# Small generators at every second unit in the linear-attention stage of a decoder step

## The chip, the cores and the metric

The kernel runs on one core of one Trainium2 chip. The time is the device time of one execution in microseconds (us), and the median over several runs counts. The profile comes from one execution of its own; times in it are counted from the start of its span.

The core has engines that run side by side, each with its own queue of instructions in fixed order: TensorE (PE in the profile; its weight loads are PEld), VectorE (DVE), ScalarE (ACT), GpSimd (POOL) and SyncE (SP), which issues DMA transfers. An instruction that has to wait holds up everything behind it on its engine.

## What is computed

One inference step of a hybrid decoder layer: an input projection that feeds two kinds of attention heads, stick-breaking attention (8 heads, with a paged cache for 8 decoding sequences of 4 tokens) and gated linear attention (4 heads or groups), a gate for each branch, and an output projection. The part that matters here is linear attention:

```python
def gla_chunk(S, q, k, v, g):
    b = jnp.cumsum(g, axis=2)
    diff = b[:, :, :, None, :] - b[:, :, None, :, :]
    decay = jnp.where(causal[None, None, :, :, None], jnp.exp(jnp.minimum(diff, 0.0)), 0.0)
    attn = jnp.einsum('bhtk,bhsk,bhtsk->bhts', q, k, decay)
    o = jnp.einsum('bhts,bhsv->bhtv', attn, v) + jnp.einsum('bhtk,bhkv->bhtv', q * jnp.exp(b), S)
    b_last = b[:, :, -1:, :]
    S_new = (jnp.exp(b_last[:, :, 0, :])[..., None] * S
             + jnp.einsum('bhsk,bhsv->bhkv', k * jnp.exp(b_last - b), v))
    return S_new, o
```

The prompt has 1024 tokens and 16 meta tokens, with 32 sample tokens behind them: T = 1072 columns. D_MODEL is 2048, a group has 128 key and 256 value columns.

## The kernel before

All projections are exact to float32 by three products: weights and activations are split into a high and a low half (wh, wl; hh, hl), and wh·hh, wh·hl and wl·hh (L288 to L290) add up in an accumulator. `inproj` (L277) projects one block of 128 columns: 8 weight chunks of 2 × 128 rows, and for each chunk 3 pieces of the 1072 tokens (384, 384, 304 columns), 6 matmuls a piece. After each piece it calls `W.beat()`: these 6 matmuls, about 1 us of TensorE, are one **unit**, and one `inproj` is 24 units. `weight_chunk` brings each chunk in: SyncE issues the load of wr, ScalarE casts it to wh (L183), VectorE subtracts to get wl (L184). After the last chunk `evac` empties the three accumulators (a pool of three buffers) through ScalarE.

All other work is woven into the projections by a `Weaver`. Work is written as Python generators; each yields the number of units until it goes on, and they lie in a heap by the unit in which they are due. `beat()` counts one unit and lets every generator that is due emit its next step, so its instructions land in the queues between two pieces of the projection. There is no other planner: the order in which instructions are emitted is the order in each engine's queue (only the weight chunks and `evac` are marked urgent).

The linear-attention stage (L644 to L1016) runs, for each of the four groups g, `inproj` for gk, gq and twice gv, 96 units in all. The three pieces of gk and gq are put into place by ScalarE copies (`place`, L672 to L680). Woven into it are, for each group:

- `decay`: for three token chunks, al on TensorE (L730), then ny, e (L733 to L737) on ScalarE and VectorE, and scans on VectorE into cb. It waits 5 units ahead of a chunk and 1 behind it.
- `own`: the diagonal blocks P_d (L754) and their masking at (L756), waiting 3 units after each.
- `level`: seven levels (64 to 1), each with X on VectorE and ScalarE (L780 to L784, the exponential in L782), 6 units later its products P (L789) and masked copies (L793, L799). `inside` starts one every 4 units.
- `inside`: after the levels, 3 units later eb, ke, k·ke (L825); 7 units later the transposes of k by token (`by_token`, L859, tr_k) and `packed` (trp_k L848, pk L849 to L851). `gv_tok` does the same for v (tr_v).
- `chunks`: 9 chunks with the state update U, the outputs o, ow (L922 to L936), then 8 samples with km (L958), Us (L961), sn (L963). Each chunk starts a `chunk_out` after 1 unit, which scales ow, waits 3 units, transposes it (otr) and writes it out through gst; at the end `samples_out` waits 9.

The next group's decay starts, and its chunks follow, once kd is there. Tiles of stages come from pools: the transposes' PSUM pool (tag tr) has one buffer, that of the P tiles two, and the stage pool `stg` seven, shared by ny, e, graw, rep, km, ow, gst, sn and the gate's gs and gx.

Two lasting generators run along: `z_feed` (VectorE products with cached key pages, L386, 2048 of them over the kernel, one step every 2 units), and `weight_forms` (L400 to L416). The groups are followed by two gate groups (`gate_group`) and `W.drain()` at L1016. The projection of further gate columns goes on after that beside the paged decode's beginning: there spn, spb (L1079), Cs (L1097) and Cn (L1101) belong to the new keys, ds_l (L1047) and a scan (L1121) to the cached ones.

Of the kernel before, what the change touches and what calls it, by code (L numbers as in the profile page):

```python
# [50 lines left out]
class Weaver:  # L51
# [1 line left out]


    def __init__(self):
        self.now, self.n, self.live, self.heap, self.mark = 0, 0, 0, [], None

    def spawn(self, gen, delay=0, lasting=False):
        heapq.heappush(self.heap, (self.now + delay, self.n, gen, lasting))
# [2 lines left out]

    def beat(self):
        self.now += 1
        while self.heap and self.heap[0][0] <= self.now:
            _, _, gen, lasting = heapq.heappop(self.heap)
            self.live -= not lasting
            d = next(gen, None)
            if d is not None:
                self.spawn(gen, d, lasting)  # L70
# [12 lines left out]
def hybrid_step(ctx: ExitStack, tc: tile.TileContext, x_prompt, x_sample, cache_k, cache_v, state_gla,  # L83
# [23 lines left out]
    W = Weaver()  # L107
# [331 lines left out]
    def gate_group(g):  # L439
        def evac(c, ps, lo, hi):  # L440
            x = stage(f"gx{g}_{c}")
            evacs.append(act.copy(x[:, :hi - lo], ps).ins)  # L442
            W.spawn(gate_rest(g, lo, hi, x), 1)
        inproj(C_SG + g * P if g < 8 else C_GG + (g - 8) * P, evac, META, f"g{g}")
# [198 lines left out]


    with tc.tile_pool(name="gp", bufs=1) as gp, tc.tile_pool(name="gps", bufs=1, space=PSUM) as gps:
        XW = 9 * P
        ones = gp.tile([P, 1], F32, name="ones")
        pool.memset(ones[:], 1.0)
# [8 lines left out]
        def view(t, off, *dims):  # L657
            a = t if isinstance(t, bass.AP) else t[:]
            return bass.AP(tensor=a.tensor, offset=a.offset + off, ap=[list(a.ap[0])] + [list(d) for d in dims])
# [56 lines left out]
        def xtile(nm):  # L716
            return gp.tile([P, XW], F32, tag="X", bufs=4, name=nm)

# [29 lines left out]
        def own(g, at, kt, qt):  # L748

            for c0 in (0, EB):  # L750
                ps = gps.tile([P, 512], F32, tag="P", bufs=2, name=f"P{g}_d_{c0}")
                for i in range(4):
                    cs = slice(c0 + i * P, c0 + (i + 1) * P)
                    mm(ps[:, i * P:(i + 1) * P], kt[:, cs], qt[:, cs], start=True, stop=True)  # L754
                j = 0 if c0 == 0 else 4
                vec.tensor_tensor(at[:, j:j + 4, :], ps[:].rearrange("p (a t) -> p a t", t=P),  # L756
                                  ident[:].unsqueeze(1).to_broadcast([P, 4, P]), ALU.mult)
                yield 3
            ps = gps.tile([P, 512], F32, tag="P", bufs=2, name=f"P{g}_d_8")
            cs = slice(1024, T)  # L760
            mm(ps[:48, :48], kt[:, cs], qt[:, cs], start=True, stop=True)
            vec.tensor_tensor(at[:48, 8, :48], ps[:48, :48], ident[:48, :48], ALU.mult)
# [39 lines left out]
        def inside(g, at, kt, qt, cb, res):  # L802

            yield from own(g, at, kt, qt)
            for m in (64, 32, 16, 8, 4, 2, 1):
                W.spawn(level(g, m, at, kt, qt, cb))
                yield 4
            yield 3
            eb = xtile(f"eb{g}")
            act.activation(eb[:, :T], cb[:, :T], AF.Exp, scale=-1.0 / 16.0)  # L810
            vec.tensor_tensor(qt[:, :T], qt[:, :T], eb[:, :T], ALU.mult)
            ebl = gp.tile([P, 17], F32, tag="ebl", name=f"ebl{g}")
            vec.tensor_copy(view(ebl, 1, (-1, 2), (2, 4)), view(eb, 0, (EB + P - 1, 2), (P, 4)))
            vec.tensor_copy(ebl[:, 8:9], eb[:, REAL - 1:REAL])
            vec.tensor_copy(ebl[:, 9:17], eb[:, REAL:T].rearrange("p (b t) -> p b t", t=NT)[:, :, NT - 1])
            ke = xtile(f"ke{g}")
            full = ((EB, 2), (P, 4), (1, P))
            vec.tensor_tensor(view(ke, 0, *full), view(cb, 0, (EB + P - 1, 2), (P, 4), (0, P)), view(cb, 0, *full),
                              ALU.subtract)
            for lo, hi, w in ((1024, REAL, 16), (REAL, T, NT)):  # L820
                cv = cb[:, lo:hi].rearrange("p (c t) -> p c t", t=w)
                vec.tensor_tensor(ke[:, lo:hi].rearrange("p (c t) -> p c t", t=w),
                                  cv[:, :, w - 1:w].to_broadcast([P, (hi - lo) // w, w]), cv, ALU.subtract)
            act.activation(ke[:, :T], ke[:, :T], AF.Exp, scale=-1.0 / 16.0)
            vec.tensor_tensor(kt[:, :T], kt[:, :T], ke[:, :T], ALU.mult)  # L825
            rep_ = three(kt[:, REAL:T], f"k{g}")
            yield 7
            kd = xtile(f"kd{g}")
            pk = gp.tile([96, P], F32R, tag="pk", name=f"pk{g}")
            by_token(kt, kd, (0, 4), col, f"k{g}")  # L830
            yield 1
            by_token(kt, kd, (4, 4), col, f"k{g}")
            yield 1
            by_token(kt, kd, (8, 1), col, f"k{g}")
            res["kd"], res["ebl"], res["pk"] = kd, ebl, pk
            yield 1
            packed(rep_, pk[:], 2, f"k{g}")

        def three(src, nm):

            rep = stage(f"rep_{nm}")[:, :96]
            vec.tensor_copy(rep.rearrange("p (a t) -> p a t", a=3), src.unsqueeze(1).to_broadcast([P, 3, NSMP]))
            return rep

        def packed(rep, dst, lo, nm):

            ps = gps.tile([P, 512], F32, tag="tr", name=f"trp_{nm}")
            nc.tensor.transpose(ps[:96, :P], rep, ident[:])  # L848
            act.copy(dst, ps[:96, :P])  # L849
            ls = slice(32 * lo, 32 * lo + 32)  # L850
            vec.tensor_tensor(dst[ls], ps[ls, :P], dst[ls].bitcast(F32), ALU.subtract)  # L851

        def by_token(src, dst, gr, at_, nm):
            c0, nch = gr
            ps = gps.tile([P, 512], F32, tag="tr", name=f"tr_{nm}_{c0}")
            for i in range(nch):
                c = c0 + i
                r = P if c < 8 else 48
                nc.tensor.transpose(ps[:r, i * P:(i + 1) * P], src[:, at_(c):at_(c) + r], ident[:])  # L859
                if r < P:  # L860
                    act.copy(dst[:r, c * P:(c + 1) * P], ps[:r, i * P:(i + 1) * P])
            nf = nch if c0 + nch < 9 else nch - 1
            if nf:
                act.copy(dst[:, c0 * P:(c0 + nf) * P], ps[:, :nf * P])
# [115 lines left out]
        for g in range(GH):  # L980
# [14 lines left out]
            pool.memset(at[:48, 8, 48:76], 0.0)  # L995
            res = {}
            W.spawn(inside(g, at, kt, qt, cbs[g], res), 2)
            gv = []
            pv = gp.tile([96, DV], F32R, tag="pv", name=f"pv{g}")
# [14 lines left out]
        for g in range(3, 5):  # L1014
            gate_group(g)
        W.drain()  # L1016

    dk_cm.__exit__(None, None, None)

# [2 lines left out]
    with tc.tile_pool(name="dp", bufs=2) as dp, tc.tile_pool(name="dps", bufs=1, space=PSUM) as dps:  # L1022
# [150 lines left out]
        def sample_out(b, osb):  # L1173

            ps = dps.tile([P, 512], F32, tag="oT", name=f"oT{b}")
            for h in range(4):
                nc.tensor.transpose(ps[:, h * P:(h + 1) * P], osb[:, h * P:(h + 1) * P], ident[:])
            a = ps[:]
            for f in range(2):
                own = bass.AP(tensor=a.tensor, offset=a.offset + 48 * f, ap=[list(a.ap[0]), [P + NT, 4], [1, NT], [64, 2]])  # L1180
                vec.tensor_reduce(osmp[:, 4 * f:4 * f + 4, b * NT:(b + 1) * NT], own, mybir.AxisListType.X, ALU.add)
            return
            yield
# [359 lines left out]
def build(arrays_by_name):  # L1543
    import concourse.bacc as bacc
    nc = bacc.Bacc("TRN2", target_bir_lowering=False, num_devices=1, dynamic_dma_scratch_size=256)
    arrays, args = {}, []
    for name in _INS:
        a = arrays_by_name[name]
        arrays[f"in_{name}_dram"] = a
        args.append(nc.dram_tensor(f"in_{name}_dram", a.shape, mybir.dt.from_np(a.dtype), kind="ExternalInput").ap())  # L1550
    for i, shape in enumerate(_OUTS):
        args.append(nc.dram_tensor(f"out_{i}_dram", shape, F32, kind="ExternalOutput").ap())
    with tile.TileContext(nc) as tc:
        hybrid_step(tc, *args)
    return nc, arrays
# [8 lines left out]
```

## Time and profile before

| | us |
|---|---|
| median of 3 runs | 2113.27 (2111.09 to 2113.43) |
| the profiled execution | 2108.24 |
| its span, first to last instruction | 2106.5 |
| TensorE busy in it | 2056.2 (98%) |
| VectorE busy | 1569.7 (75%) |
| ScalarE busy | 991.8 (47%) |
| granted TensorE clock, mean | 0.995 |

The profiled execution is 0.24% below the median, and 1.7 us of it lie around the span. A matmul's duration in the timeline includes its passage through the array, so consecutive matmuls overlap; the distance between two starts is what one costs. A number in brackets at the end of a row is the idle time of the engine before it and what ended it. Line numbers with "L" are those of the kernel before; in the changed kernel they are 2 to 4 higher.

### The profile page before, as it was taken

To read this page: it belongs to the slowest core of one execution; us is meant where nothing else is said; L and a number is where in the kernel's file an instruction comes from. 1 tells how busy PE (TensorE), PEld (TensorE's weight loads), DVE (VectorE), ACT (ScalarE), POOL (GpSimd) and SP (SyncE) were. 2 spreads that over 40 slices of the span, in tenths; PEclk is the share of its full clock that TensorE was granted. 3 is DMA by queue.
4 is the path that set the end of the run, shared out by engine and by line. 5 is a ranking of instruction groups with operands and counts; after the bars stand their busy time and mean duration, and the time that the engine had idled before them with its cause. 6 is when DMAs were issued, how large, how long until landed. Compare 5 with 4: busy or idle time off the path is not lost.

```text
span 2106.5 us, 43298 instructions
## 1 busy us (share of the span) xinstructions
PE 2056.2 (98%) x12546; PEld 1868.4 (89%) x12546; DVE 1569.7 (75%) x6593; ACT 991.8 (47%) x2539; POOL 80.9 (4%) x298
## 2 busy tenths in 40 slices
PE   5999999999999999999999999999999999999998
PEld 4999999999999989999899898998888888777776
DVE  6368888889888889899889988877544347453576
ACT  7346555565655547423535335353444326332342
POOL 0000000100000000020000000000000000000000
PEclk9999999999999999999999999999999999999999
DMA  6234443544444353544353444434776666352485
GB/s 200 72 103 123 132 131 100 144 118 121 139 124 126 108 145 102 156 132 117 110 138 104 123 129 113 107 85 135 244 234 219 224 218 201 127 159 75 130 279 186
DMA packets 378505, 301.96 MB, mean 143 GB/s; under 512 B 50073, under 2 KB 318777, under 8 KB 378265
## 3 DMA queue, kind: packets, MB, share of 16 engines
q1 hardware_dynamic: 376072, 298.91, 48.1%
q8 instruction: 99, 1.62, 0.3%
q14 instruction: 142, 1.16, 0.2%
q10 hardware_dynamic: 2192, 0.27, 0.1%
HBM read 241.75 MB, written 57.31 MB: 142 GB/s over the span
## 4 chain that ended last, share of the span: by engine, by line
PE 84%; DMA 6%; DVE 6%; ACT 2%; issue 1%; SPq 0%; DVEq 0%; POOL 0%; ACTq 0%; POOLq 0%
PE acc_g L288 4%; PE acc_g L290 4%; PE b L1471 4%; PE acc_g L289 4%; PE b L1472 4%; PE b L1473 4%; PE acc_k L288 3%; PE acc_gv L288 3%; PE acc_k L289 3%; PE acc_q L288 3%; PE acc_k L290 3%; PE acc_gv L290 3%; PE acc_gv L289 3%; PE acc_q L289 3%; PE acc_q L290 3%; PE acc_v L288 3%
## 5 line engine op out<-in xcount | busy, mean ns | idle before, releaser
L386 DVE SCALAR_TENSOR_TENSOR jk<-kp,qb 128x128 f32<-128x128 f32 x2048 | 591.6, 289 | 38.9 <-DMA qb<-qsd 1.5
L288 PE MATMUL acc_g<-hT,wh_g 128*128 128x368 f32 (+2 forms) x768 | 251.7, 328 | 0.8 <-ACT gx L442 0.8
L290 PE MATMUL acc_g<-hT,wl_g 128*128 128x368 f32 (+2 forms) x768 | 248.4, 323 | 0.0
L289 PE MATMUL acc_g<-hT,wh_g 128*128 128x368 f32 (+2 forms) x768 | 247.9, 323 | 0.0
L1471 PE MATMUL b<-ring,f 128*128 128x512 f32 x416 | 165.7, 400 | 3.2 <-ACT b L1344 2.0
L386 DVE DVE_READ_ACCUMULATOR jk<-kp,qb 128x1 f32 x2048 | 166.9, 81 | 0.0
L1309 DVE TENSOR_TENSOR ring<-wr,ring 128x512 fp32r<-128x512 f32 x104 | 70.6, 690 | 128.7 <-ACT ring L1308 128.3
L1472 PE MATMUL b<-ring,f 128*128 128x512 f32 x416 | 162.8, 391 | 0.7 <-DVE ring L1309 0.5
L1473 PE MATMUL b<-ring,f 128*128 128x512 f32 x416 | 162.4, 390 | 0.0
L288 PEld LDWEIGHTS acc_g<-hT,wh_g 128*128 128x128 f32 x768 | 145.1, 189 | 12.4 <-issue 10.2
L290 PEld LDWEIGHTS acc_g<-hT,wl_g 128*128 128x128 f32 x768 | 144.9, 189 | 2.0 <-issue 2.0
L289 PEld LDWEIGHTS acc_g<-hT,wh_g 128*128 128x128 f32 x768 | 145.1, 189 | 0.7
L1308 ACT CAST ring<-wr 128x512 fp32r<-128x512 f32 x104 | 64.4, 622 | 159.0 <-DMA wr<-in_w_out_dram 80.6
L288 PE MATMUL acc_gv<-hT,wh_gv 128*128 128x384 f32 (+1 forms) x384 | 129.6, 338 | 0.0
L288 PE MATMUL acc_k<-hT,wh_k 128*128 128x378 f32 (+1 forms) x384 | 127.8, 333 | 0.0
L288 PE MATMUL acc_q<-hT,wh_q 128*128 128x368 f32 (+2 forms) x384 | 125.5, 327 | 0.0
L289 PE MATMUL acc_k<-hT,wh_k 128*128 128x378 f32 (+1 forms) x384 | 125.5, 327 | 0.0
L290 PE MATMUL acc_k<-hT,wl_k 128*128 128x378 f32 (+1 forms) x384 | 125.3, 326 | 0.0
L290 PE MATMUL acc_gv<-hT,wl_gv 128*128 128x384 f32 (+1 forms) x384 | 125.2, 326 | 0.0
L289 PE MATMUL acc_gv<-hT,wh_gv 128*128 128x384 f32 (+1 forms) x384 | 124.6, 325 | 0.0
L289 PE MATMUL acc_q<-hT,wh_q 128*128 128x368 f32 (+2 forms) x384 | 123.8, 322 | 0.0
L290 PE MATMUL acc_q<-hT,wl_q 128*128 128x368 f32 (+2 forms) x384 | 123.6, 322 | 0.0
(441 smaller groups left out, 5398.3 us busy)
## 6 DMA issues: line engine op xcount, KB each, us to landing
kp<-in_cache_k_dram SPq DMA_DIRECT2D x512, 64.0 KB
vr<-in_cache_v_dram SPq DMA_DIRECT2D x64, 512.0 KB
tf<-in_w_out_dram SPq DMA_DIRECT2D x64, 256.0 KB
qb<-qsd SPq DMA_DIRECT2D x64, 256.0 KB
td<-tf SPq DMA_DIRECT2D x64, 256.0 KB
wr_g<-in_w_in_dram SPq DMA_DIRECT2D x128, 128.0 KB
wr<-td SPq DMA_DIRECT2D x64, 256.0 KB
wr<-in_w_out_dram SPq DMA_DIRECT2D x48, 256.0 KB
```

The source lines that it names most:

```text
L288: mm(acc[c][:, :n], wh[:, k2, :], hh[k][:, lo:hi], start=(k == 0), stop=False)
L289: mm(acc[c][:, :n], wh[:, k2, :], hl[k][:, lo:hi], start=False, stop=False)
L290: W.mark = mm(acc[c][:, :n], wl[:, k2, :], hh[k][:, lo:hi], start=False, stop=(k == NK - 1)).ins
L386: ins = vec.scalar_tensor_tensor(jk[:], kp[:], 1.0, qbs[h, b][:, t, :], ALU.mult, ALU.mult, accum_out=zt[:, t, NPG - 1 - i:NPG - i])
L1308: act.copy(wh, r)
L1309: vec.tensor_tensor(wl, r, wh.bitcast(F32), ALU.subtract)
L1471: mm(bk[:], ah, wh, start=first and k == 0, stop=False, skip_group_check=True)
L1472: mm(bk[:], ah, wl, start=False, stop=False, skip_group_check=True)
L1473: mm(bk[:], al, wh, start=False, stop=last and k == 7, skip_group_check=True)
```

## The change

The Weaver gets a `stride`. `beat()` still counts every unit, but lets generators go on only in units that are multiples of the stride. It is 2 in the linear-attention stage and 1 elsewhere. A generator that is due in an odd unit goes on in the next even one: waits of 1, 3, 5 and 9 become 2, 4, 6 and 10 where they begin in an even unit. `z_feed` (2) and the levels (4 and 6) keep theirs. Three waits in `own` and `inside`, which belong to the scores' generator, are one unit less: 3 to 2, 3 to 2, 7 to 6. No instruction is added or removed on any engine, and kd is ready at the same unit in every group.

```diff
@@ class Weaver
     def __init__(self):
-        self.now, self.n, self.live, self.heap, self.mark = 0, 0, 0, [], None
+        self.now, self.n, self.live, self.heap, self.mark, self.stride = 0, 0, 0, [], None, 1
...
     def beat(self):
         self.now += 1
+        if self.now % self.stride:
+            return
         while self.heap and self.heap[0][0] <= self.now:
             _, _, gen, lasting = heapq.heappop(self.heap)
             self.live -= not lasting
...
     with tc.tile_pool(name="gp", bufs=1) as gp, tc.tile_pool(name="gps", bufs=1, space=PSUM) as gps:
+        W.stride = 2
         XW = 9 * P
@@ own
                 vec.tensor_tensor(at[:, j:j + 4, :], ps[:].rearrange("p (a t) -> p a t", t=P),
                                   ident[:].unsqueeze(1).to_broadcast([P, 4, P]), ALU.mult)
-                yield 3
+                yield 2
@@ inside
                 W.spawn(level(g, m, at, kt, qt, cb))
                 yield 4
-            yield 3
+            yield 2
             eb = xtile(f"eb{g}")
...
             rep_ = three(kt[:, REAL:T], f"k{g}")
-            yield 7
+            yield 6
             kd = xtile(f"kd{g}")
...
         for g in range(3, 5):
             gate_group(g)
         W.drain()
+        W.stride = 1
```

The first place is ScalarE where gk of group 0 is emptied (acc_gk is the accumulator, its three pieces 0 to 2; wh_gq the next block's weights; ny, e the decay's; X_64 the first level's). Before:

```order
L733 ACTIVATE ny_2_16425<-al_2_16423,nbal 128x304
L724 COPY wal_18130<-walr 96x128
L735 ACTIVATE e_2_16426<-e_2_16426 128x304
L736 ACTIVATE e_2_16426<-e_2_16426 128x304
L183 COPY wh_gq_1_16638<-wr_gq_1_16636 128x256
L672 COPY gk_16028<-acc_gk_0_16030 128x256
L673 COPY gk_16028<-acc_gk_0_16030 128x128
L675 COPY gk_16028<-acc_gk_1_16031 128x256
L676 COPY gk_16028<-acc_gk_1_16031 128x128
L782 ACTIVATE X_64_17177<-X_64_17177 128x1024
L678 COPY gk_16028<-acc_gk_2_16032 128x128
L679 COPY gk_16028<-acc_gk_2_16032 128x128
```

And after, on the same engine at the same place:

```order
L185 COPY wh_gq_1_16619<-wr_gq_1_16617 128x256
L675 COPY gk_16028<-acc_gk_0_16030 128x256
L676 COPY gk_16028<-acc_gk_0_16030 128x128
L678 COPY gk_16028<-acc_gk_1_16031 128x256
L679 COPY gk_16028<-acc_gk_1_16031 128x128
L185 COPY wh_gq_2_16683<-wr_gq_2_16681 128x256
L681 COPY gk_16028<-acc_gk_2_16032 128x128
L682 COPY gk_16028<-acc_gk_2_16032 128x128
L683 COPY gk_16028<-acc_gk_2_16032 128x48
L736 ACTIVATE ny_2_16520<-al_2_16518,nbal 128x304
L727 COPY wal_18112<-walr 96x128
L738 ACTIVATE e_2_16521<-e_2_16521 128x304
```

The third piece of the decay (ny_2, e_2) has moved from ahead of the copies of gk to behind them, and the exponential of X_64 no longer stands between them.

The second place is VectorE in group 0's second gv block, around its last low half of weights, wl_gv_1_7 (k·ke is written gk<-gk,ke). Before:

```order
L793 COPY_PREDICATED at_17012<-lvl_16482,P_1_17845 128x256
L184 TENSOR_TENSOR wl_gv_1_7_18008<-wr_gv_1_7_18005,wh_gv_1_7_18007 128x256
L386 TENSOR_SCALAR jk_5_5_2_17798,zt_5_17563<-kp_5_5_17552,qb_5_17310 128x128
L793 COPY_PREDICATED at_17012<-lvl_16482,P_1_17845 128x256
L386 TENSOR_SCALAR jk_5_5_3_17800,zt_5_17563<-kp_5_5_17552,qb_5_17310 128x128
L799 COPY_PREDICATED at_17012<-lvl_16482,P_1_8_17852 48x24
```

And after:

```order
L796 COPY_PREDICATED at_17012<-lvl_16588,P_1_17789 128x256
L388 TENSOR_SCALAR jk_5_4_2_17773,zt_5_17586<-kp_5_4_17521,qb_5_17335 128x128
L802 COPY_PREDICATED at_17012<-lvl_16588,P_1_8_17796 48x24
L388 TENSOR_SCALAR jk_5_4_3_17775,zt_5_17586<-kp_5_4_17521,qb_5_17335 128x128
L828 TENSOR_TENSOR gk_16028<-gk_16028,ke_17806 128x1072
L388 TENSOR_SCALAR jk_5_5_0_17825,zt_5_17586<-kp_5_5_17575,qb_5_17335 128x128
L845 COPY rep_k_17812<-gk_16028 128x96
L388 TENSOR_SCALAR jk_5_5_1_17827,zt_5_17586<-kp_5_5_17575,qb_5_17335 128x128
L186 TENSOR_TENSOR wl_gv_1_7_18003<-wr_gv_1_7_18000,wh_gv_1_7_18002 128x256
```

The last masked copies of level 1, k·ke and rep_k now stand ahead of wl_gv_1_7; before they stood behind it.

The third place is VectorE at the new keys of the paged decode, behind the stage. Before:

```order
L1071 TENSOR_TENSOR spn<-spn,nmask 32x32
L184 TENSOR_TENSOR wl_g_0_27125<-wr_g_0_27122,wh_g_0_27124 128x256
L1079 TENSOR_TENSOR spb<-spn,bmask 32x256
L1047 TENSOR_TENSOR ds_l<-ds_26970,ds_h 128x256
L1121 TENSOR_SCALAR ds_26970<-sm_26807,ds_26970 128x256
```

And after:

```order
L186 TENSOR_TENSOR wl_g_0_27125<-wr_g_0_27122,wh_g_0_27124 128x256
L1045 TENSOR_TENSOR spn<-zn,spn 32x32
L1051 TENSOR_TENSOR ds_l<-ds_26970,ds_h 128x256
L1075 TENSOR_TENSOR spn<-spn,nmask 32x32
L1125 TENSOR_SCALAR ds_26970<-sm_26807,ds_26970 128x256
L1083 TENSOR_TENSOR spb<-spn,bmask 32x256
```

The tile spb, which TensorE's Cs reads, now stands behind ds_l and the scan.

## The prediction

> **What bounds the kernel now.** I read the page's busy shares first, then the page's chain, then the busy times by stage, and after that the timelines of the places where TensorE waits.
>
> ```profile
> span 2106.5 us, 43298 instructions
> PE 2056.2 (98%) x12546; PEld 1868.4 (89%) x12546; DVE 1569.7 (75%) x6593; ACT 991.8 (47%) x2539; POOL 80.9 (4%) x298
> PE 84%; DMA 6%; DVE 6%; ACT 2%; issue 1%; SPq 0%; DVEq 0%; POOL 0%; ACTq 0%; POOLq 0%
> ```
>
> TensorE is busy for 2056.2 of 2106.5 us and holds 84% of the chain that ended last. The change adds and removes no instruction, so what it can win or lose are TensorE's waits inside the linear-attention stage, its turns between main work and small work, and what the stage leaves to its successor. The view of busy time by windows (length, then TensorE, its weight loads, VectorE, ScalarE, GpSimd, granted clock, DMA share, GB/s) gives the stage's groups 0 to 3:
>
> ```profile
> 905.00:1035.00 130.00, 126.35 (x854) 120.09 (x853) 120.48 (x611) 56.62 (x162) 2.97 (x6) 0.99 0.42 116
> 1035.00:1166.00 131.00, 129.40 (x871) 120.36 (x870) 116.27 (x588) 55.63 (x167) 0.23 (x2) 1.00 0.44 123
> 1166.00:1296.00 130.00, 129.74 (x873) 120.85 (x872) 115.45 (x585) 54.43 (x165) 0.18 (x2) 1.00 0.42 117
> 1296.00:1425.00 129.00, 129.00 (x879) 120.56 (x871) 106.86 (x567) 52.45 (x157) 0.18 (x2) 1.00 0.40 106
> ```
>
> Only group 0 has more than 2 us without TensorE work (130.00 − 126.35 = 3.65); groups 1 to 3 have 1.6, 0.3 and 0.0. So a large gain from waits can only come from group 0. VectorE is the next bound, at 120.48 of 130 us there.
>
> **Group 0: the evacuation of gk.** The waits of TensorE around 905 us, in the view of waits:
>
> ```profile
> PE acc_gq L288 <- ACT gk L673: 2.2, 1, 2.2
> PE acc_gq L288 <- ACT gk L680: 1.2, 1, 1.2
> ```
>
> Both are waits for ScalarE to empty an accumulator of gk0. ScalarE's and TensorE's timelines (start, duration, engine, line) say why it is late:
>
> ```profile
> 906.79 0.46 ACT L735 ACTIVATE e<-e 128x304 f32<-128x304 f32 x1 [5.20 <-issue]
> ...
> 907.94 0.36 ACT L672 COPY gk<-acc_gk 128x256 f32<-128x256 f32 x1
> ...
> 911.82 1.06 ACT L782 ACTIVATE X<-X 128x1024 f32<-128x1024 f32 x1 [2.92 <-DVE X L781]
> 912.79 0.25 ACT L678 COPY gk<-acc_gk 128x128 f32<-128x128 f32 x1
> ```
> ```profile
> 906.06 0.30 PE L290 MATMUL acc_gk<-hT,wl_gk 128*128 128x304 f32 x1
> 908.52 0.45 PE L288 MATMUL acc_gq<-hT,wh_gq 128*128 128x384 f32 x1 [2.16 <-ACT gk L673]
> ...
> 911.64 0.52 PE L290 MATMUL acc_gq<-hT,wl_gq 128*128 128x384 f32 x1
> 913.35 0.41 PE L288 MATMUL acc_gq<-hT,wh_gq 128*128 128x304 f32 x1 [1.19 <-ACT gk L680]
> ```
>
> ScalarE stands 5.20 us before e (chunk 2 of the decay), which waits for VectorE; the copies of gk (L672 on) are queued behind it. Then X, which waits 2.92 us for VectorE, stands ahead of the last copies (L678 on). How the sizes come out needs the ordinary distance between two matmuls, from a quiet place with one turn to small work in it:
>
> ```profile
> 955.04 0.31 PE L290 MATMUL acc_gv<-hT,wl_gv 128*128 128x304 f32 x1
> 955.19 1.06 PE L789 MATMUL P<-X 128*128 128x128 f32 x8
> 956.00 0.42 PE L288 MATMUL acc_gv<-hT,wh_gv 128*128 128x384 f32 x1
> 956.26 0.34 PE L289 MATMUL acc_gv<-hT,wh_gv 128*128 128x384 f32 x1
> 956.43 0.34 PE L290 MATMUL acc_gv<-hT,wl_gv 128*128 128x384 f32 x1
> ```
>
> From 956.26 to 956.43 is 0.17 us (0.14 for the narrow chunk). So the first wait costs 908.52 − 906.06 − 0.14 = 2.32 us and the second 913.35 − 911.64 − 0.17 = 1.54. Between them, eleven distances take 911.64 − 908.52 = 3.12 us in place of 11 × 0.17 = 1.87: another 1.25 us, since the clock was halved right after the first wait:
>
> ```profile
> 909.00:912.00 3.00, 3.00 (x11) 2.66 (x9) 3.00 (x14) 0.18 (x1) 0.00 (x0) 0.54 0.31 91
> ```
>
> In all 2.32 + 1.54 + 1.25 = 5.1 us. [...]
>
> The change takes both causes away. At every second unit, decay's waiting time of 5 becomes 6, so chunk 2's e now comes behind all of gk0's copies, and X of level 64 does too: the rows of ScalarE in the section on the change show it. Nothing in the copies' way then waits for VectorE. What is late next is VectorE's low half of the weights, wl. VectorE has no gap at the group's middle (9.93 of 10 us in the view by windows), and what fills it are the page products, 0.289 + 0.081 = 0.37 us each in the page's groups:
>
> ```profile
> L386 DVE SCALAR_TENSOR_TENSOR jk<-kp,qb 128x128 f32<-128x128 f32 x2048 | 591.6, 289 | 38.9 <-DMA qb<-qsd 1.5
> L386 DVE DVE_READ_ACCUMULATOR jk<-kp,qb 128x1 f32 x2048 | 166.9, 81 | 0.0
> ```
> ```profile
> 975.00:985.00 10.00, 10.00 (x68) 9.69 (x67) 9.93 (x38) 2.36 (x4) 0.00 (x0) 1.00 0.32 100
> ```
> ```profile
> 945.58 0.42 DVE L184 TENSOR_TENSOR wl_gv<-wr_gv,wh_gv 128x256 fp32r<-128x256 f32 x1
> 948.82 0.34 PE L290 MATMUL acc_gv<-hT,wl_gv 128*128 128x384 f32 x1
> ...
> 984.10 0.45 DVE L184 TENSOR_TENSOR wl_gv<-wr_gv,wh_gv 128x256 fp32r<-128x256 f32 x1
> 987.52 1.27 DVE L825 TENSOR_TENSOR gk<-gk,ke 128x1072 f32<-128x1072 f32 x1
> 989.67 0.34 PE L290 MATMUL acc_gv<-hT,wl_gv 128*128 128x384 f32 x1
> ```
>
> At 945.58 + 0.42 = 946.00 the low half is done that TensorE takes at 948.82: 2.8 us in hand. In the new order that subtraction stands two rows earlier, which at a page product each (2 × 0.37 = 0.7) makes 3.5. The last one of the group has 989.67 − 984.55 = 5.1 in hand, but now kt·ke (1.27) and small rows worth two page products (0.7) more stand ahead of it: 5.1 − 2.0 = 3.1. A VectorE without gaps does not come earlier because TensorE does, so TensorE can keep no more than about 3.1 to 3.5 of the 5.1. I take **−3.3**, bounds −5.1 (VectorE gets ahead) and −2.8 (as it was at 948.82).
>
> **Turns to small work.** At 956.00 the first matmul after the small ones holds TensorE for 0.26 instead of 0.17, and the last one before is 0.01 to 0.04 longer: about 0.12 us a turn. Counted in the order of TensorE, the stage has 149 runs of small work instead of 161, as two units' work now goes together: 12 × 0.12 = **−1.4**. Bounds −1.6 and 0 (if the longer runs make the wait on each other's PSUM buffer).
>
> **Transposes, group 1.** The pool of the transposes has one buffer, so tr_v waits until pk has been read by VectorE:
>
> ```profile
> 1128.03 0.30 PE L290 MATMUL acc_gk<-hT,wl_gk 128*128 128x304 f32 x1
> 1129.02 0.55 PE L859 MATMUL tr_v<-ident,graw 128*128 128x128 f32 x3 [0.69 <-DVE pk L851]
> ```
>
> That costs 0.99 − 0.14 = 0.85. Now eight matmuls of 0.17 stand between the two instead of six of 0.14: 0.5 us more cover. Bounds −0.9 and 0; I take **−0.7**, between the 0.5 of cover and the whole.
>
> **Leaving the stage: new keys (Cs).** The gate projection runs on into the paged decode. TensorE waits there for spb, in the chain and in VectorE's timeline:
>
> ```profile
> 1475.64 2.32 issue
> 1477.96 0.67 PE Cs L1097 x2
> ```
> ```profile
> 1477.46 0.41 DVE L1079 TENSOR_TENSOR spb<-spn,bmask 32x256 f32<-32x256 f32 x1
> 1477.79 0.60 DVE L1047 TENSOR_TENSOR ds_l<-ds,ds_h 128x256 fp32r<-128x256 f32 x1
> 1478.42 0.69 DVE L1121 TENSOR_TENSOR_SCAN ds<-sm,ds 128x256 f32<-128x256 f32 x1
> ```
>
> Now Cs stands six matmuls later on TensorE (about 1.0 us of cover), but on VectorE ds_l (0.60) and the scan (0.69) stand ahead of spb instead of behind it, and the page products end a unit later, of which two (0.7) still lie ahead of it. 0.60 + 0.69 + 0.7 − 1.0 = 1.0, and **+1.1** with the turn that falls later; bounds −0.5 (the products are not in the way) and +2.2 (none of the cover helps).
>
> **Edits that I cost at nothing.** The shorter waits in own and inside (3 to 2, 3 to 2, 7 to 6) only make up for the rounding to even units; kd is ready at the same unit in each group, so no group begins later. The DMAs of the weights, states and outputs are issued in the same number; SP moves by at most a unit (1.36 us, from 130 us for a group's 96), and the DMA share of 0.40 to 0.44 leaves room for it. What would appear if this cover went is the first rival below.
>
> **Sum.** −3.3 − 1.4 − 0.7 + 1.1 = −4.3 us. The rows are from the profiled execution of 2108.24 us (span 2106.5, and 1.7 around it), which would become 2103.9. It lies 5.0 below the median of the runs, 2113.27; taken from that, **2109.0**. 0.2% is 4.2 us, about what a measurement of this kernel can tell from no change, so the sum lies on that edge.
>
> **The rivals.**
>
> *Slower: the stage pool of seven buffers.* chunk_out waits 1 and 3 units, now 2 and 4, so each output tile ow is held for six units instead of four, one buffer more at any time while chunks run; km, sn, gst and gs take from the same pool. One wait of that kind is in the trace, km held up by gs until its transfer:
>
> ```profile
> 1433.38 0.28 DVE L958 TENSOR_SCALAR km<-pk,rmask 96x128 fp32r<-96x128 f32 x1 [1.78 <-DMA md<-gs]
> 1433.71 0.38 PE L961 MATMUL Us<-pv,km 96*128 96x256 f32 x1 [1.54 <-DVE km L958]
> ```
>
> At 1.7 us each, five more of them (4.3 + 4.2 = 8.5) bring the time past +0.2%; two in each group, eight, give −4.3 + 13.6 = +9.3, so 2122.6. Against it: there is only one such wait of that size now, with nine chunks in each of four groups. Chance 0.18.
>
> *All of the 5.1 is kept.* VectorE's page products are cheap to overtake, and Cs stays: −5.1 − 1.4 − 0.7 = −7.2, 2106.1. Against it: the row of 9.93 busy in 10. [...] Chance 0.18.
>
> *Bunches on VectorE give it back.* What came at two units comes at one, so each low half of weights can stand behind twice the work; where 5.1 in hand fell to 3.1 in group 0, the others fall alike, and a wait of about 0.8 (as the tr_v one) in each of four groups costs 3.2: −4.3 + 3.2 = −1.1, 2112.2. For it: VectorE is at 116.27 of 131 and 115.45 of 130; against: waits there are nearly nil now. It takes in the case that TensorE is held elsewhere for the same time, and so that nothing changes. Chance 0.22.
>
> **How the numbers follow.** My forecast, whose own range I put at −2 to −6.5 inside the sum of the bounds (−0.6 to −8.1), has 0.42: about 0.28 of that lies beyond −0.2% and 0.14 within. With the 0.18 of the full gain, faster is 0.46; within 0.2% is 0.14 + 0.22 = 0.36; slower 0.18. The range goes from 2102 (the full gain, 2106.1, and below it by the 4.2 that a measurement can't tell) to 2118 (the slower case with about half of its eight waits, 2109.0 + 5 × 1.7 = 2117.5), leaving out about 2 in 10.
>
> **What would show it.** Right: the two waits for gk at L673 and L680 and the half clock at 909 are gone; group 0 takes about 127 us; the wait at Cs is 3.4 us; fewer, longer runs of small matmuls. Wrong: waits for wl in group 0, waits of Us for km with a transfer named in groups 1 to 3, or a half clock at a new place.

## The result

The changed kernel takes 2114.84 us (median of 14 runs, 2113.16 to 2119.9) where the kernel before takes 2111.73 in the same comparison (14 runs, 2107.02 to 2116.59): ratio 1.0016, 95% interval 1.0009 to 1.0024. It is slower by about 3.1 us (by the medians; 3.4 by the ratio), inside the 0.2% that the prediction took for its edge, and on the other side of no change: 4.3 us less was forecast. That 2114.84 lies in the range of 2102 to 2118 says only that the range was wide. One execution of a later kernel (2988.4 us, granted clock 0.695) and one of the kernel before (10205.77 us) lie far outside all others and are in no ratio.

The page of the changed kernel, profiled in an execution with a span of 2111.5 us (before 2106.5):

```profile
span 2111.5 us, 43349 instructions
PE 2057.4 (97%) x12546; PEld 1870.9 (89%) x12546; DVE 1566.5 (74%) x6593; ACT 992.5 (47%) x2539; POOL 80.6 (4%) x298
PE 83%; DVE 7%; DMA 6%; issue 2%; ACT 1%; SPq 0%; DVEq 0%; ACTq 0%; POOL 0%; POOLq 0%
```

The 51 instructions more are semaphore waits, which no engine counts as busy. TensorE does the same work in the same time; the chain has 7% of VectorE instead of 6% and 83% of TensorE instead of 84%. Its windows for the four groups and the waits of TensorE in group 0 answer to those shown of the kernel before:

```profile
905.00:1035.00 130.00, 124.85 (x821) 118.72 (x819) 115.99 (x598) 52.87 (x157) 4.55 (x10) 0.99 0.43 113
1035.00:1166.00 131.00, 128.03 (x849) 120.15 (x850) 114.13 (x581) 54.48 (x162) 0.23 (x2) 1.00 0.42 120
1166.00:1296.00 130.00, 128.39 (x865) 120.44 (x864) 114.76 (x585) 55.06 (x164) 0.24 (x2) 1.00 0.43 117
1296.00:1425.00 129.00, 128.95 (x871) 120.90 (x871) 109.98 (x576) 54.08 (x161) 0.24 (x2) 1.00 0.39 106
```
```profile
PE P_d L764 <- DVE at L759: 2.2, 1, 2.2
PE tr_v L862 <- ACT gv L867: 1.3, 1, 1.3
PE otr L887 <- ACT gst L889: 0.5, 1, 0.5
PE acc_gq L292 <- DVE wl_gq L186: 0.4, 1, 0.4
PE acc_gq L290 <- ACT wh_gq L185: 0.3, 1, 0.3
PE acc_gq L290 <- ACT gk L676: 0.2, 1, 0.2
```

The waits for gk are down from 2.2 and 1.2 us to 0.2. In their place TensorE waits for VectorE's mask of the diagonal tiles (P_d for at), for a ScalarE copy (tr_v for gv), and for halves of the weights (wl_gq, wh_gq). Group 0 has 5.15 us without TensorE work (130.00 − 124.85), where it had 3.65; groups 1 and 2 have 3.0 and 1.6, where they had 1.6 and 0.3.

When TensorE starts the same projection matmul in the two profiles shows where time went. The table is worked out from the two timelines. Where small work stands at different places in the two kernels, the difference swings by 1 us and more between the rows. The two profiles are 5.0 us apart and the medians 3.1, so about 2 us of the last rows belong to these two executions.

| place | before | after | difference |
|---|---|---|---|
| end of gk0 | 905.02 | 904.41 | −0.61 |
| gq0, behind the old waits for gk | 913.35 | 908.31 | −5.04 |
| gq0, 10 us on | 923.00 | 919.63 | −3.38 |
| gv0, ahead of P_d_8 | 941.32 | 938.42 | −2.90 |
| gv0, behind P_d_8 and the half clock | 944.62 | 945.44 | +0.81 |
| gv1 of group 0, behind tr_v | 982.58 | 985.06 | +2.48 |
| end of group 0 | 1035.55 | 1037.74 | +2.18 |
| early in group 2 | 1167.84 | 1171.71 | +3.87 |
| gate, end of the groups | 1393.35 | 1398.60 | +5.25 |
| last before Cs | 1475.12 | 1479.25 | +4.13 |
| behind Cs | 1485.38 | 1489.89 | +4.51 |

The relief came, 4.4 us from the first row to the second. In the next 10 us 1.7 of it went back: TensorE came to three new chunks of wl and one of wh before they were ready. The longest of these waits, first VectorE's row and then TensorE's:

```profile
916.04 0.40 DVE L186 TENSOR_TENSOR wl_gq<-wr_gq,wh_gq 128x256 fp32r<-128x256 f32 x1
916.50 0.44 PE L292 MATMUL acc_gq<-hT,wl_gq 128*128 128x384 f32 x1 [0.41 <-DVE wl_gq L186]
```

The matmul starts 0.06 us behind the end of the subtraction (916.44), and those of the chunks before and behind it start 0.05 to 0.06 us behind theirs. Ahead of P_d_8, at 941 us, 2.3 of the 4.4 were left (−0.61 to −2.90). By the middle of group 0's last block it was gone and 3.1 us more with it (−0.61 to +2.48); the later groups added some 3 us, and the gate's beginning gave 1 back.

The largest loss, in TensorE's timeline and then VectorE's of the changed kernel (the page products between VectorE's rows are left out):

```profile
939.11 0.30 PE L292 MATMUL acc_gv<-hT,wl_gv 128*128 128x304 f32 x1
941.59 0.29 PE L764 MATMUL P_d<-gq,gk 128*48 128x48 f32 x2 [2.18 <-DVE at L759]
941.81 0.44 PE L290 MATMUL acc_gv<-hT,wh_gv 128*128 128x384 f32 x1
```
```profile
938.40 0.69 DVE L786 TENSOR_TENSOR X<-X,gq 128x512 f32<-128x512 f32 x1
939.22 0.68 DVE L786 TENSOR_TENSOR X<-X,gq 128x512 f32<-128x512 f32 x1
940.03 0.68 DVE L786 TENSOR_TENSOR X<-X,gq 128x512 f32<-128x512 f32 x1
940.85 0.68 DVE L759 TENSOR_TENSOR at<-P_d,ident 128x512 f32<-128x512 f32 x1
```

P_d_8 is the third of own's tiles and takes the P buffer of the first, which VectorE empties with its mask (L759) at 940.85, behind three X. TensorE stands 2.3 us, and then has half its clock (granted clock 0.50 in the second window, 13 matmuls in 3.4 us):

```profile
938.86:942.27 3.41, 1.23 (x9) 0.93 (x9) 3.41 (x13) 0.41 (x1) 0.00 (x0) 1.00 0.44 123
942.30:945.70 3.40, 3.40 (x13) 3.40 (x12) 3.19 (x20) 0.00 (x0) 0.00 (x0) 0.50 0.30 82
```

VectorE was busy for all 3.41 us of the wait. The second loss is tr_v, in ScalarE's timeline:

```profile
968.88 1.14 ACT L785 ACTIVATE X<-X 128x1120 f32<-128x1120 f32 x1 [3.07 <-DVE X L784]
969.93 0.39 ACT L185 CAST wh_gv<-wr_gv 128x256 fp32r<-128x256 f32 x1
970.22 0.47 ACT L867 COPY gv<-tr_v 128x384 f32<-128x384 f32 x1
```

The copy that empties the only buffer of the transposes stands behind X, and X waits 3.07 us for VectorE. In the kernel before that copy (at 964.71) stood ahead of its X (at 965.15). So this wait, too, is VectorE's, by way of ScalarE's new order.

### The profile page after: what moved, and what is told of

Read it like the earlier page. It is cut to its first block, busy times and chain, and to the rows that moved or that the text cites. A ratio compares the mean times of both kernels' runs of the same rounds, so it can differ in the third digit from the quotient of the medians.

```text
span 2111.5 us, 43349 instructions
## 1 busy us (share of the span) xinstructions
PE 2057.4 (97%) x12546; PEld 1870.9 (89%) x12546; DVE 1566.5 (74%) x6593; ACT 992.5 (47%) x2539; POOL 80.6 (4%) x298
## 4 chain that ended last, share of the span: by engine, by line
PE 83%; DVE 7%; DMA 6%; issue 2%; ACT 1%; SPq 0%; DVEq 0%; ACTq 0%; POOL 0%; POOLq 0%
PE acc_g L290 5%; PE acc_g L291 5%; PE acc_g L292 5%; PE b L1475 4%; PE b L1476 4%; PE b L1477 4%; PE acc_k L290 3%; PE acc_k L291 3%; PE acc_q L290 3%; PE acc_k L292 3%; PE acc_q L291 3%; PE acc_q L292 3%; PE acc_v L290 3%; PE acc_v L292 2%; PE acc_v L291 2%; DVE jk L388 2%
```

## The experiments

Times are ratios to the kernel before, measured on the same chip in the same rounds; 0.001 is 2.1 us. Differences in the sections are worked out from the ratios. The kernels were not all timed in one comparison; the changed kernel's 1.0016 is that of the result. The medians of all runs give ratios that differ from these by up to 0.001 (0.9986 instead of 0.9976 for own's wait alone), so less than about 2 us between two kernels is not told apart.

### Each of the two waits taken away alone

One kernel gives P_d_8 of group 0 a buffer of its own, the changed kernel with this edit:

```diff
-            ps = gps.tile([P, 512], F32, tag="P", bufs=2, name=f"P{g}_d_8")
+            ps = gps.tile([P, 256], F32, tag="U", name=f"P{g}_d_8") if g == 0 else gps.tile([P, 512], F32, tag="P", bufs=2, name=f"P{g}_d_8")
```

> The changed kernel, but in group 0 the last diagonal tile P_d_8 comes from the idle buffer of U, not from the two P buffers, so it need not wait until VectorE has masked the first P_d. Theory A (what group 0 won at gk0 was lost at P_d_8: a wait of 2.3 us and the halved clock behind it, about 1.6 us): the wait is gone and the time is about 3.9 us lower than that of the changed kernel, which is about 0.6 us below the kernel before. Rival B (VectorE alone sets the pace of group 0): TensorE waits elsewhere for the low halves of weights instead, and no more than 1 us is won, so it stays 2 us or more above the kernel before.

Measured: 1.0016 (1.0006 to 1.0027), the same as the changed kernel. The waits of TensorE between 935 and 985 us in its profile:

```profile
PE tr_v L862 <- ACT gv L867: 3.2, 1, 3.2
PE P L801 <- DVE at L796: 1.9, 1, 1.9
```

The wait at P_d_8 is gone, and what it won came back within 40 us: tr_v waits 3.2 instead of 1.3, and a level's P for a VectorE copy 1.9. That is rival B.

The other spreads the transposes of v, in the changed kernel:

```diff
                 rep = three(raw[:, REAL - lo:T - lo], f"v{g}_{f}")
-            yield 2
+            yield 4 if c == 2 else 2
```

> The changed kernel, but the third piece of gv waits 4 units and not 2 before its transposes, so that the second and third no longer fall together. Theory A (tr_v waits for ScalarE's copy of the tr_v before it, 1.3 us in group 0, 1.8 in two places and some more in groups 1 to 3): these waits are gone, and the time is about 3 us lower than that of the changed kernel, about as long as the kernel before. Rival B (the waits only move on to the next transposes, or cost nothing since VectorE is the bound): less than 1 us lower, 2 us or more above the kernel before.

Measured: 1.0015 (1.0005 to 1.0024), again no difference to the changed kernel. In its profile tr_v's wait for ScalarE is gone in group 0 and P_d_8 waits as before; in group 1 tr_v waits 2.2 us for pk instead of 1.5. So the time speaks for rival B; its profiled execution alone (span 2109.2, the fastest of its runs) would have spoken for A.

Both edits together:

> The changed kernel with both repairs, P_d_8 of group 0 in the idle buffer of U and the third piece of gv 4 units later. Each alone moved the median by no more than 0.4 us. Theory A (VectorE is the bound of group 0, so that a wait taken away comes back as the next): at the end of group 0 TensorE is no more than 1 us ahead of the kernel before, and the time is within 2 us of the changed kernel. Rival B (the two waits hid each other): with both gone TensorE keeps 3 us of the gain at gk0, and the time is 4 us or more below the changed kernel, below the kernel before.

Measured: 1.0010 (1.0000 to 1.0020). Group 0 of its profile still has these:

```profile
PE tr_v L862 <- ACT gv L867: 2.0, 1, 2.0
PE P L801 <- DVE at L796: 1.9, 1, 1.9
```

From 877 us to the end of group 0 TensorE takes 2.6 us longer than in the kernel before (a difference of −0.20 at 877 and +2.42 at 1035.55); the time of the kernel before there holds the half clock at 909 us (0.54 from 909 to 912). Theory A holds: a wait taken away comes back as the next one.

### VectorE made cheaper in group 0

```diff
                 jk = dk.tile([P, P], F32, tag="jk", bufs=1, name=f"jk{b}_{h}_{i}_{t}")
-                ins = vec.scalar_tensor_tensor(jk[:], kp[:], 1.0, qbs[h, b][:, t, :], ALU.mult, ALU.mult,
+                w = 32 if 640 <= W.now < 736 else P
+                ins = vec.scalar_tensor_tensor(jk[:, :w], kp[:, :w], 1.0, qbs[h, b][:, t, :w], ALU.mult, ALU.mult,
```

> The changed kernel with the page products of group 0's units 640 to 735 taken over 32 columns in place of 128 (it leaves out three quarters of those products; order and number of instructions stay). Theory A (VectorE is the bound of group 0): with about 40 us less to do there, the waits of P_d_8 and tr_v in group 0 and the halved clock go, and the gain of about 5 us at gk0 is kept: the time is 6 us or more below that of the changed kernel. Rival B (single PSUM buffers and the order on ScalarE make the waits): P_d_8 and tr_v still wait above 1 us each, less than 3 us are won.

Measured: 0.9977 (0.9964 to 0.9990), 0.0039 or 8 us below the changed kernel. Its window of group 0 and the waits of TensorE in it:

```profile
905.00:1035.00 130.00, 128.25 (x875) 122.99 (x874) 104.33 (x609) 56.91 (x169) 4.82 (x10) 1.00 0.42 117
```
```profile
PE acc_gq L290 <- ACT gk L684: 1.2, 1, 1.2
PE otr L888 <- ACT gst L890: 0.5, 1, 0.5
```

The order of instructions is that of the changed kernel, the buffers too; only VectorE has less to do (104.33 us in the window instead of 115.99; 188 products take 0.19 instead of 0.29 each, so some 19 us less and not 40 as expected). P_d_8, tr_v and the matmuls of wl do not wait any more, the granted clock is 1.00 in the window, and TensorE ends group 0 at 1032.09 us, 3.5 ahead of the kernel before and not 2.2 behind. Single buffers and ScalarE's order are where the waits show; VectorE's load is what makes them in group 0. In groups 1 and 2, where the products are as before, tr_v waits as in the changed kernel (1.8 us in all for gv, 1.5 for pk). The gain includes the removed work only as far as TensorE waited for it, since TensorE's own work is unchanged. The same cut was not tried in the kernel before, so how much of the 8 us it would win without the change is not known.

### The two halves of the change

The three shorter waits alone, in the kernel before:

```diff
-                yield 3
+                yield 2
...
-            yield 3
+            yield 2
             eb = xtile(f"eb{g}")
...
-            yield 7
+            yield 6
             kd = xtile(f"kd{g}")
```

> The kernel before with only the three waits of own and inside one unit shorter, every unit used. Theory A (the stride makes the bunches, and without it the shorter waits cost little): within 1.5 us of the kernel before, the waits for gk0 at 906 and 912 us still there, no wait at P_d_8 above 1 us. Rival B (the shorter waits alone bring tiles ahead of what VectorE can deliver): a wait of 2 us at P_d_8 with a halved clock, 3 us or more slower than the kernel before.

Measured: 0.9969 (0.9958 to 0.9980), faster than both kernels by 0.003 and more. Neither theory had that. In its profile the waits for gk0 are there (2.9 and 0.9), and P_d_8 does not wait. The gain does not lie in group 0: TensorE is 2.4 us later than in the kernel before at its end (1035.55), 0.6 earlier at the end of the groups (1393.35) and 2.4 earlier at 1475.

The stride alone, in the changed kernel with the waits back at 3, 3 and 7:

> The changed kernel with the three waits put back to 3, 3 and 7, so the stride alone; rounded, they are 4, 4 and 8. Theory A (the two parts add up: the changed kernel is 3.1 above the kernel before, the three waits alone 6.1 below): the stride alone costs about 9, in the same waits as the changed kernel (tr_v, one or two in each group) and, since kd comes up to eight units later, in units without a projection at the end of each group; P_d_8 has two more units and does not wait. Rival B (the parts do not add up; the shorter waits are only good with every unit used): within 2 us of the changed kernel.

Measured: 1.0002 (0.9990 to 1.0014). Theory A, which had 9 us more, is out; rival B is right that the parts do not add up, though the time is 3 us below the changed kernel and not within 2: 0.9969 and 1.0002 would make 0.9971, the changed kernel has 1.0016. With every unit used the shorter waits win 6.5 us; under the stride they win nothing, and the point estimates say that they lose 3. The profile of the stride alone has no wait at P_d_8 but one of 3.5 us at tr_v. (The execution that was profiled took 2115.59 us, 2.6 more than the median of 2112.96, so its waits can't be set against the time.)

Then the three waits apart. own's alone, and inside's two alone, both in the kernel before:

> The kernel before with own's wait 2 instead of 3 and nothing else: levels, k-transposes and kd come two units earlier. Theory A (the gain of the three waits comes from kd and its transposes leaving the units in which the v pieces are emptied and transposed): part of the 6 us, 2 to 4 us below the kernel before. Rival B (the gain is that of inside's two waits): within 1 us of the kernel before.

> The kernel before with only inside's waits of 2 and 6 instead of 3 and 7: the k-transposes and kd come two units earlier, own and the levels stay. Theory A (the gain comes from the k-transposes being earlier, by any of the three waits): 2 to 4 us below the kernel before, the wait of tr_v for pk in group 1 (0.7 us) gone. Rival B (the gain is own's): within 1 us of the kernel before.

Measured: own's 0.9976 (0.9965 to 0.9986), inside's 1.0011 (1.0001 to 1.0021). The gain comes with own's wait; inside's by themselves cost a little and, going by the points, help a little on top of it (0.9969, inside the noise). The mechanism of theory A falls in both, since inside's also bring the k-transposes two units forward and do not win. Why own's wins 5 us (3 by the medians) is not settled. A part can be read: the wait of Us for km behind the gate's buffers, 1.5 us at 1432 before, is 0.3 in the profile of own's, 1.7 in that of inside's, and none in that of all three.

### The relief at gk0 by itself

decay's waits as the stride rounds them, in the kernel before:

```diff
-                yield 5
+                yield 6
...
-                yield 1
+                yield 2
```

> The kernel before with one thing changed: decay waits 6 and 2 units instead of 5 and 1, every unit is used. Theory A (the emptying of gk0 was held up by the decay's third piece): the waits for gk at 906 and 912 us go, 5.1 us are won there, and since P_d_8 has 2.1 us in hand before VectorE's mask, 2 to 3 us of them are kept. Rival B (VectorE, without a gap, gives nothing): all 5.1 come back as waits in group 0, and the time is within 1 us of the kernel before. If all of the 5.1 is kept, VectorE was no bound.

Measured: 0.9990 (0.9980 to 1.0000), so about 2 us faster, as theory A has it, though the interval ends at no change. Group 0's waits in its profile:

```profile
PE trp_v L848 <- ACT gv L864: 2.1, 1, 2.1
PE acc_gq L290 <- DVE wl_gq L184: 1.5, 2, 1.1
```

The waits for gk are gone, P_d_8 (own's wait still 3) does not wait, and most of the 5 us comes back as waits for wl and at trp_v. With the three shorter waits on top:

> The kernel before with the three shorter waits and with decay's waits of 6 and 2, every unit used. Theory A (the two gains, 6.1 and 1.6, add up): about 7.7 us below the kernel before. Rival B (with P_d_8 a unit or two earlier and TensorE 5 us further at gk0, P_d_8 waits for VectorE's mask as in the changed kernel, 2 us and a halved clock): no faster than the three waits alone, 2 to 6 below the kernel before.

Measured: 0.9971 (0.9959 to 0.9982), no faster than the three waits alone, as rival B has it:

```profile
PE P_d L761 <- DVE at L756: 2.2, 1, 2.2
PE trp_v L848 <- ACT gv L864: 2.0, 1, 2.0
PE acc_gq L290 <- DVE wl_gq L184: 1.1, 1, 1.1
```

So the wait at P_d_8 needs both parts of the change: it is there with own's wait of 2, which puts P_d_8 four units behind the first P_d instead of six, and gk0 relieved (this kernel and the changed one), and absent with own's wait of 3 (decay alone), or with own's wait of 2 and gk0 still late (the three waits alone).

The same run shows that group 0 is not the whole account. It has the waits of 2.2 us at P_d_8 and 2.0 at the transposes, and TensorE ends group 0 2.7 us later than in the kernel before, where the changed kernel is 2.2 later; yet it is 6 us faster than the kernel before and the changed kernel 3 slower. In the profiles they part behind group 0: from there to the end of the groups this kernel wins 1.1 us and the changed one loses 3.1.

At last the same with part of VectorE's work moved out of group 0:

```diff
-        W.spawn(z_feed(lambda n: 2), lasting=True)
+        W.spawn(z_feed(lambda n: 3 if 284 <= n < 316 else 1 if n >= 364 and n % 4 == 0 else 2), lasting=True)
```

> The three shorter waits and decay's 6 and 2 (every unit used), and the page products at every third unit in group 0, made up for from group 2 on: 16 pages, about 24 us of VectorE, leave group 0. Theory A (VectorE is what ate the gain at gk0 when decay's waits were added): the waits of P_d_8 (2.2 us) and trp_v (2.0 us) in group 0 fall below 1 us, and the time is 3 us or more below the three waits with decay alone, so 9 or more below the kernel before. Rival B (what leaves group 0 makes waits in groups 2 and 3, where VectorE has 15 to 20 us to spare): within 2 us of the three waits with decay alone.

Measured: 1.0000 (0.9990 to 1.0010). Group 0 did as theory A says, and no wait is left in it; behind it, where the products that were put off fall, more was lost than had been won. Windows of groups 0, 2 and 3, and TensorE's largest waits from 1166 to 1490 us:

```profile
905.00:1035.00 130.00, 129.71 (x884) 124.47 (x883) 109.69 (x530) 58.56 (x173) 3.62 (x8) 1.00 0.39 109
1166.00:1296.00 130.00, 126.30 (x836) 118.45 (x834) 119.46 (x632) 54.51 (x160) 0.12 (x1) 1.00 0.43 117
1296.00:1425.00 129.00, 128.03 (x852) 120.31 (x852) 114.40 (x621) 52.82 (x157) 0.24 (x2) 1.00 0.44 110
```
```profile
PE Us L961 <- DVE km L958: 2.5, 1, 2.5
PE otr L884 <- ACT gst L886: 2.2, 3, 1.5
```

At 109.69 of 130 us VectorE is in nobody's way in group 0. In group 2, at 119.46 of 130, TensorE stands 3.7 us (0.3 in the kernel before), and in group 3, at 114.40 of 129, it stands 1.0 (0.0). The wait of 2.5 us at Us lies behind the groups. Both theories hold, each in its groups, and the second decides the time.

### The kernel before once more

> The kernel before, unchanged, for a second profile: its first one is 3.5 us below the median of its runs. Theory A (the halved clock falls behind more of its waits in other executions, as after the 1.9 us wait at 881 us or after the one of 1.7 at 1432): the second profile has the same waits and one more stretch of half clock, about 1.7 us each. Rival B: it has longer waits elsewhere. If it is near 2108 again, nothing is told apart.

Measured: one execution of 2116.13 us, span 2114.3, 7.8 us longer than the first profile of the same program. A part lies in half clock: from 886.3 to 889.7 us it is 0.51, behind the wait of 1.9 us for gx, where the first profile has 1.00 (last section). Over the whole execution the mean granted clock is 0.994 instead of 0.995. Another part is spread over waits that are somewhat longer, among them 1.2 us near 775 us, 0.5 at gk0 (1.4 and 2.5 where it had 2.2 and 1.2) and 0.9 around Cs. So both theories are right in part.

## Why the prediction was wrong

**The bound and the first wait: right.** TensorE was the bound, and group 0 the only place with a gain. The waits for gk at L673 and L680 and the half clock at 909 went, and the place gave 4.4 us of the 5.1. Of the 5.1, 1.25 was half clock, and not every wait had that behind it: the one of 1.8 us at 882 in the same profile had none (last section).

**What group 0 keeps: the step that failed.** The prediction said that "A VectorE without gaps does not come earlier because TensorE does", and then asked this of one consumer only, wl, and found 3.1 to 3.5 us in hand. As far as it went this was right: TensorE came into the first gv block 3 us earlier, yet VectorE's first seven subtractions for it came between 0.2 us earlier and 0.4 later than before, and the waits for wl and wh had cut the gain to 2.8 us at 923. They fell in gq, though, some 30 us ahead of the row that the prediction had looked at. But TensorE reads VectorE's results at other places too. P_d_8 needs the mask of the first P_d: TensorE came early there and stood. tr_v needs a copy that now stands on ScalarE behind an X which VectorE makes; there TensorE was already late and stood again. The term of −3.3 measured +3.1 at the last block of group 0, and group 0, from the end of gk0 to the same place of the next gk, takes 133.3 us instead of 130.5, and not the 127 of the forecast. The runs that took one wait away, then the other, then both, moved the time by no more than the noise, and the one that made VectorE's products cheaper brought 8 us; so the cap in group 0 was VectorE's load, as the prediction's rule had it, and the error was to look for it in one row.

**Groups 1 to 3: no term for new waits.** The prediction took from the busy times that these groups had nothing to win, and its main sum lets them lose nothing; only the rival of the bunches had a price for it. They lost 3.1 us in the profile. Its waits there are 1.8 us at tr_v for gv, 1.5 at tr_v for pk and 1.2 at otr, where the kernel before has 0.7 for pk, 0.6 for a DMA and 0.5 at otr. The kernels with the same shorter waits but without the stride win there instead. Which of the waits that the stride rounds up makes the difference was not separated.

**"Edits that I cost at nothing": failed in the same place.** The shorter waits were said to "only make up for the rounding". With own's wait of 2 P_d_8 comes closer behind the tile whose buffer it takes, and together with the relief at gk0 that is the wait of 2.2 us, with 1.4 us of half clock behind it in this profile. Alone, with every unit used, the same three edits win 6.5 us, which no term of the sum held.

**Turns to small work: right in kind.** Between gk0's end and the gate there are 147 turns instead of 158, and each costs 0.08 us behind it: −0.9 and not −1.4.

**Transposes of group 1: wrong.** Eight matmuls in place of six gave no cover: the wait for pk is 1.5 instead of 0.7 us. On VectorE a wl_gk (0.42) and rep_v (0.24) now stand shortly ahead of pk; before, both were done 2.6 us or more ahead of it. There is also a wait of 0.9 at tr_v in each of groups 1 and 2 that was not there before. The term of −0.7 measured about +1.7 for group 1.

**Cs: too large.** +1.1 was forecast; the gap ahead of Cs grew from 2.5 to 2.8 us (in the timelines 1477.96 − 1475.29 − 0.17 and 1483.36 − 1480.42 − 0.14), +0.3.

**The rivals.** That bunches on VectorE give the gain back is what happened, though it had 1.1 us below the kernel before and 3.1 above was measured; its price, 0.8 in each group, was near for groups 1 to 3 (3.1 together) and far too low for group 0. The stage pool did not do it: from start to start the wait of Us for km fell from 1.7 to 0.8 us. That all is kept fell with the first rows.

**The scale.** The sum was of the size of the differences between two executions of one program: the profile it was made on lies 7.8 us below the second profile of the same kernel.

## What to carry to other kernels

When an engine is relieved of a wait, ask of every result that it takes from the next-busiest engine, not of the one with the most rows, how many microseconds it has in hand; the smallest of these caps the gain, and here the wait of 2.2 us at P_d_8 cost another 1.4 in clock. If taking a wait away only brings up the next one, make the suspected engine's work cheaper for a look: if the waits go together, that engine makes them, though here its busy share was 89%. Two edits of one change should be timed apart when they touch the same buffers: here the one that was meant as an adjustment was the better half.

## What the runs showed of the hardware

The same wait had half clock behind it in one execution and none in another. The kernel before waits for gx at 882 us, 1.8 us in its first profile and 1.9 in its second. In the first TensorE is idle for 0.29 and 1.47 us of the first two windows, and the granted clock is 1.00 in all three:

```profile
878.50:881.90 3.40, 3.11 (x20) 2.79 (x18) 3.23 (x18) 0.63 (x2) 0.00 (x0) 1.00 0.34 89
881.90:885.30 3.40, 1.93 (x12) 1.94 (x13) 3.26 (x20) 2.83 (x8) 0.00 (x0) 1.00 0.56 131
885.30:888.70 3.40, 3.40 (x23) 3.40 (x22) 1.60 (x7) 1.24 (x4) 0.00 (x0) 1.00 0.67 190
```

In the second it is idle for 1.94 of the first 3.50 us, and the clock is 0.51 in the next 3.40, with 13 matmuls where the first profile has 23:

```profile
882.80:886.30 3.50, 1.56 (x10) 1.24 (x9) 3.33 (x22) 1.11 (x4) 0.00 (x0) 0.99 0.41 104
886.30:889.70 3.40, 3.40 (x13) 3.40 (x14) 3.00 (x15) 2.74 (x8) 0.00 (x0) 0.51 0.45 117
```

The wait of 2.2 us at P_d_8 in the changed kernel's profile (2.18 us idle) has a clock of 0.50 behind it, from 942.30 to 945.70 us, which cost 1.4 us there (3.7 from −2.90 to +0.81 in the table, less the 2.3 of the wait). In the first profile of the kernel before, the wait of 2.2 us at gk0 (2.16 us idle) has 0.54 behind it, from 909 to 912 us, which cost 1.25. What decides whether a wait has half clock behind it was not tested, and how much of the 9.6 us over which the runs of the kernel before spread is the clock, no run shows.
